# Block inverses of a chunked RWKV-7 recurrence: lower-left parts packed four to a product, and rows taken when a bank is emptied

## The chip, the cores and the metric

The kernel runs on one core of one Trainium2 chip. The metric is the device time of one execution in microseconds. A core has a matrix engine (PE, with its weight loads shown apart as PEld), a vector engine (DVE), a scalar engine (ACT), GpSimd (POOL) and SyncE (SP). PE multiplies a stationary operand of up to 128x128 (the weights) with a moving operand and writes to PSUM, which has eight banks of 128 x 512 fp32 here; the other operands live in SBUF, 128 partitions wide. In this kernel SP does nothing but issue DMAs. Each engine takes its instructions in order.

## What is computed

One step of a hybrid decoder layer on 1024 prompt tokens and 8 sample tokens (one new token each), model width 1024, fp32 throughout. A projection `p = x @ w_in` gives the rows of two branches and their gates. One branch is gated linear attention with 4 heads. The other is RWKV-7 with 16 heads of width 64, a recurrence over tokens:

```
def step(S, inp):
    rt, wt, kt, vt, kkt, at = inp
    sa = einsum('bhvk,bhk->bhv', S, -kkt)
    S = S * wt[:, :, None, :] + sa[..., None] * (kkt * at)[:, :, None, :] + vt[..., None] * kt[:, :, None, :]
    y = einsum('bhvk,bhk->bhv', S, rt)
    return S, y
...
m = sigmoid(gate_a) * (o_gla @ w_up_gla) + sigmoid(gate_b) * (o_rwkv @ w_up_rwkv)
y_out = layernorm(ALPHA * x + m @ w_out)
```

Both branches are normalised and gated before the up-projections, and the new states are outputs too.

## The kernel before

**Two passes.** The tokens are taken in two passes of 512 prompt tokens each (`PASS`); the first also carries the 8 sample tokens (520 columns, as two tiles of 260), the second is one tile of 512. In each pass a long list of *blocks* is worked off (`make_plan`, `blocks`): a block is one 128-column slice of a weight matrix times all tokens of the pass, in 8 slices of depth and three matmuls each (high and low halves of weights and tokens: `whi`, `wlo`, `xh`, `xl`). So a tile of a block is 24 matmuls into one PSUM bank, and the bank is emptied by an *evacuation* (`evacuate`, with the function `ev` that the block's `act` has returned) into a row buffer in SBUF. There are 26 row buffers of 128 x 520, in the pool `row`. Weights are loaded, split on ACT and DVE, and in the first pass their halves are also stored to DRAM, from where the second pass loads them (`load_w`).

**A planner writes the order.** Every piece of work is a generator (a stream) that yields operations or conditions. `Order.run` picks, operation by operation, the one that can start first by its own table of costs and priorities, and emits it; the order on each engine is fixed that way when the kernel is built. `get` and `row` make a stream wait in the planner until a buffer is free: `row(n, KEEP)` waits until one more row is idle than others ask for. Banks are shared out in the same way: two for `proj`, three `big`, one `pch`, two `pY`; up-projections may take any of `proj`, `pY` and `big` (`get_of`).

**Where a block gets its row.** `gla_row` (line 751), `lora` (938), `rwkv_row` (1014) and `gate_row` (1358) are the `act` of a block. Each takes its row before it returns `ev`, and `blocks` (677) runs `act` before the block's first matmul. `up_row` (1392) is the `act` of an up-projection: it waits until a gate has been loaded (`self.gts`, filled by `load_gates`) and takes it off the list, also before the first matmul.

**A pair of heads.** RWKV is worked by pairs of heads, 8 in each pass, 16 in all (`pair`, line 1019): `front`, `back`, `turn`, `chain`, `norm`. Each pass has 8 chunks of 64 tokens (`NCH`). `front` (1034) builds the chunk matrices in `GG` and inverts, for each chunk and head, a unit triangular 64 x 64 matrix. It does so in blocks of 32: the diagonal blocks are written from `GG` to DRAM (`LD`, four DMAs), read back so that each partition holds one block (`L_`, four DMAs named `wide<-LD` in the profile), and solved by 31 steps on DVE (`X`, with `Xt` between). The result goes to DRAM (`XD`, four DMAs) and from there to the diagonal of `XT` (four DMAs, `XT<-XD`). A pair has 8 chunks x 2 heads = 16 such matrices, so 32 solved blocks.

**The lower-left parts.** `back` (1141) computes the off-diagonal block of each inverse from the two diagonal inverses and the off-diagonal block of `GG`, in two rounds of products. The first multiplies, chunk by chunk, the whole of `GG[:, x, 0]` (128 x 128, both heads) with the transposed blocks `X1`; of each result only the rows of interest are copied to `As`. The second multiplies `As` with the other diagonal blocks in `XT`. Each round is 8 products with 128 x 128 weights and 64 moving columns, since a chunk's two heads take two columns of 32 and only one quadrant of 32 partitions of each is used. In the profile the first round has the name `big<-X,gg` and the second `big<-XT,As`. At the end `GG`'s first half is overwritten from `AZ` for `chain`, which runs over the 8 chunks in order.

`X1` and `As` are fixed buffers (line 545), zeroed once at the start, one of each.

Of the kernel before, what the change touches and what calls it, by code (L numbers as in the profile page):

```python
# [20 lines left out]
P = 128  # L21
# [28 lines left out]
    "sto": ([P, P], 1), "bnd": ([P, 1], 3), "st": ([P, 32], 3), "part": ([P, HALF], 2), "l2p": ([P, 2 * P], 2),  # L50
    "pair": ([P, 2, HT // 32], 3),
}
PARTS = ("part", "l2p")
# [29 lines left out]
SETS = {AF.Sigmoid: SIGMOID, AF.Tanh: SIGMOID, AF.Exp: EXP, AF.Ln: EXP}  # L83

HS = (slice(0, 64), slice(64, 128))
LEVELS = [1, 2, 4, 8, 16, 32, 64]
MASKED = 4
GLA_EPS = 1e-5
# [314 lines left out]
class Kern(Order):  # L403
# [71 lines left out]
    def setup(self):  # L475
# [63 lines left out]
        for t in self.Sp:  # L539
            nc.gpsimd.memset(t, 0.0)  # L540

        for tag, n, bufs in (("az", 4 * HT, 2), ("XT", 2 * HT, 2), ("X1", HT, 1), ("As", 2 * HT, 1)):
            ts = [cp.tile([P, n], F32, name=f"{tag}{i}") for i in range(bufs)]
            for t in ts:
                nc.gpsimd.memset(t, 0.0)
            self.fixed(tag, ts)
# [78 lines left out]
    def load_w(self):  # L625

        H = NK // 2
        todo = [(b.src, b.c0, j, b.c.i) for b in self.plan if b.src is not None for j in range(2)]
        raws, his, los, kept = [], [], [], {}

        def keep(src, c0, j, hi, lo):
            for v, x in zip("hl", (hi, lo)):
                t = self.dr.tile([P, 512], F32, name=f"w{v}{c0}_{j}")
                kept.setdefault((c0, j), []).append(t)
                yield self.S.dma_start(t, x.bitcast(F32))

        def high():
            n = 0
            while True:
                yield lambda: len(raws) > n  # L640
                hi = yield from self.get("whi")
                yield self.A.copy(hi, raws[n][0])
                his.append(hi)
                n += 1
                if n == count:
                    return

        def low():
            for n in range(count):
                yield lambda: len(his) > n  # L650
                lo = yield from self.get("wlo")
                raw, src, c0, j, i = raws[n]
                yield self.E.tensor_sub(lo, raw, his[n].bitcast(F32))
                self.free(raw)
                los.append(lo)
                if src is self.a["w_in"] and i == 0:
                    yield from keep(src, c0, j, his[n], lo)
                self.ws.append((his[n], lo))
            self.w_done = True
        count = sum(src is not self.a["w_in"] or i == 0 for src, _, _, i in todo)  # L660
        self.spawn(high(), "w")
        self.spawn(low(), "w")
        for n, (src, c0, j, i) in enumerate(todo):
            if src is self.a["w_in"] and i:
                yield lambda: len(los) == len(raws)
                hi, lo = (yield from self.get("whi")), (yield from self.get("wlo"))
                for x, t in zip((hi, lo), kept[c0, j]):
                    yield self.S.dma_start(x.bitcast(F32), t)
                self.ws.append((hi, lo))
                continue  # L670
            raw = yield from self.get("wraw")
            op = self.S.dma_start(raw.rearrange("p (k c) -> p k c", c=P),
                                  src[j * H * P:(j + 1) * H * P, c0:c0 + P].rearrange("(k p) c -> p k c", p=P))
            yield from self.load(f"w{n}", op)
            raws.append((raw, src, c0, j, i))

    def blocks(self):
        xs = None
        for b in self.plan:
# [5 lines left out]
            if b.src is None:  # L685
                yield from b.act(xs)
                xs = None
                continue
            evac = yield from b.act()
            w = []  # L690
            tiles = b.c.tiles
            for tt, (t0, n) in enumerate(tiles):
# [28 lines left out]
    def low_rank(self, c, raws, used):  # L721
# [26 lines left out]
            c.alr_ready += 1  # L748
        self.free(x_)

    def gla_row(self, c, rows, scale):
        x = yield from self.row(c.n, KEEP)
        rows.append(x)

        def ev(tt, t0, w, q):
            yield self.A.activation(x[:, t0:t0 + w], q, AF.Copy, scale=scale)
        return ev

# [177 lines left out]


    def lora(self, c):
        c.lraw = yield from self.row(c.n)
        return self.shift(c, 32, c.lraw, c.lraw[:, HT:])  # L940

    def lora_done(self, c):
        def parts():
# [40 lines left out]
    def shift(self, c, j, dst, smp):  # L984
# [4 lines left out]
        edge = {}  # L989

        def ev(tt, t0, n, q):
            np_ = n - c.ns if tt == last else n
            yield lambda: "pv" in self.has
# [12 lines left out]
            if prev is not None:  # L1006
                yield V.scalar_tensor_tensor(dst[:, t0:t0 + 1], prev, mu, dst[:, t0:t0 + 1], ALU.mult, ALU.add)
                if not i:
                    self.free(prev)
            if i == 0 and tt == last:  # L1010
                yield V.scalar_tensor_tensor(smp, self.shT[:, j], mu, dst[:, HT:c.n], ALU.mult, ALU.add)
        return ev

    def rwkv_row(self, c, rows, n, p):
        x = yield from self.row(c.n, KEEP)
        rows.append(x)
        return self.shift(c, 8 * n + p, x, self.smp[:, n, p])

    def pair(self, c, p, st, gate):
        d = SimpleNamespace()  # L1020
# [13 lines left out]
    def front(self, c, p, st, d):  # L1034
# [73 lines left out]
        for q in range(2):  # L1108
            b = slice(32 * q, 32 * q + 32)
            for h in range(2):  # L1110
                yield self.S.dma_start(LD[2 * q + h].rearrange("c s t -> s c t"), GG[HS[h]][b, :, 0, h, b])
        L = L_.rearrange("p (s t) -> p s t", t=32)
        X_ = yield from self.get("X")
        X = X_.rearrange("p (i t) -> p i t", t=32)
# [18 lines left out]
        for q in range(2):  # L1133
            b = slice(32 * q, 32 * q + 32)
            for h in range(2):
                n = 2 * q + h
                yield self.S.dma_start(XT[HS[h]][b, :, h, b], XD[n * NCH:(n + 1) * NCH].rearrange("c s t -> s c t"))
        d.AZ, d.BK, d.G, d.XT, d.v, d.bonus, d.pc, d.L = AZ, BK, GG, XT, st[2], st[1], pc, L_
        d.y = Pc_[:, :HT]
# [24 lines left out]

    def turn(self, d):

# [189 lines left out]


    def gate_row(self, c, n, x):
        gt = yield from self.row(c.n, KEEP)

        def ev(tt, t0, w, q):
            yield self.A.copy(gt[:, t0:t0 + w], q)
            if tt == len(c.tiles) - 1:
                yield self.S.dma_start(self.sg[c.i][n][x], gt)
# [225 lines left out]
    def run_all(self):  # L1590
# [4 lines left out]
        self.plan, self.xq, self.ws, self.wo, self.gts = [], [], [], [], []  # L1595
# [65 lines left out]
```

## Time and profile before

| what | value |
|---|---|
| time, median of 3 runs | 1655.22 us (1649.95 to 1656.4) |
| span of the profiled execution, first to last instruction | 1647.8 us |
| mean granted PE clock in it | 0.995 |
| HBM read, written | 195.45 MB, 117.82 MB |
| matmul instructions of the first and of the second round in back | 256 and 256 |

The profile page and all answers of the trace are of one profiled execution. The page gives its span and no time around it, so the runs' times stand beside it and are not of the same execution. In rows of groups, the columns are engine, operation, output and inputs, tile, shape and count, then busy time in us and mean ns of one, then the engine's idle time before them and who ended it. Every instruction that the planner emits has the line of its emitter, L215, so groups go by the names of tiles. Matmul durations overlap their followers; the pace is read from starts. A row of waits is: total us, times, longest us.

### The profile page before, as it was taken

The page shows a single profiled execution, that of the slowest core. Times are in us where ns is not written, and L with a number is a line of the kernel's source. Part 1 is how long each engine was busy: PE and PEld are TensorE (multiplying, and loading weights), DVE is VectorE, ACT ScalarE, POOL GpSimd, SP SyncE. Part 2 cuts the span into 40 slices and gives each one's busy share as a digit, 9 for nine tenths or more (in the row PEclk, how much of TensorE's full clock was granted, in tenths as well). Part 3 has the DMA queues.
Part 4 walks back from the last instruction along what each step waited for, and adds up shares of the span by engine and source line. Part 5 has one row for each costly group of instructions (what it writes and reads, how often), then busy time and mean ns, then how long its engine had stood idle before and what let it go on. Part 6 is the DMA issues. An engine that isn't in the chain of part 4 may idle for free.

```text
span 1647.8 us, 30094 instructions
## 1 busy us (share of the span) xinstructions
PE 1604.5 (97%) x10322; PEld 1422.9 (86%) x10322; DVE 1234.7 (75%) x3187; ACT 844.6 (51%) x2015; POOL 103.3 (6%) x192
## 2 busy tenths in 40 slices
PE   8999999999999999999999999999999999999998
PEld 7899999999999988788878787888788889988786
DVE  6787887788878887768678888796767775665565
ACT  5546755656476646553635462536345645554210
POOL 1100100100000000000001011100000000000000
PEclk9999999999999999999999999999999999999999
DMA  8878764696569655645465546544653577798432
GB/s 281 263 220 254 222 204 149 197 301 198 176 193 280 213 181 189 206 162 145 134 178 162 147 141 193 180 129 125 207 147 106 172 227 228 242 292 264 151 109 84
DMA packets 311925, 315.28 MB, mean 191 GB/s; under 512 B 75364, under 2 KB 197357, under 8 KB 311773
## 3 DMA queue, kind: packets, MB, share of 16 engines
q1 hardware_dynamic: 311772, 313.36, 61.2%
q8 instruction: 82, 1.34, 0.3%
q14 instruction: 71, 0.57, 0.1%
HBM read 195.45 MB, written 117.82 MB: 190 GB/s over the span
## 4 chain that ended last, share of the span: by engine, by line
PE 71%; DVE 13%; DMA 7%; ACT 3%; SPq 3%; issue 2%; POOL 0%; POOLq 0%; DVEq 0%; ACTq 0%
PE proj L215 39%; PE big L215 22%; PE pY L215 7%; PE pch L215 4%; DVE row L215 4%; SPq L215 3%; DVE X L215 2%; DVE Xt L215 2%; DMA wide<-LD 2%; ACT row L215 1%; DVE wide L215 1%; DVE wlo L215 1%; DVE pair L215 1%; DMA whi<-wh 1%; DMA l2s<-lora 1%
## 5 line engine op out<-in xcount | busy, mean ns | idle before, releaser
L215 PE MATMUL proj<-xh,whi 128*128 128x260 f32 (+1 forms) x1872 | 618.2, 330 | 0.1
L215 PE MATMUL proj<-xh,wlo 128*128 128x260 f32 (+1 forms) x1872 | 615.8, 329 | 0.5 <-POOL wlo L215 0.5
L215 PE MATMUL proj<-xl,whi 128*128 128x260 f32 (+1 forms) x1872 | 612.9, 327 | 0.8 <-DVE xl L215 0.7
L215 PEld LDWEIGHTS proj<-xh,wlo 128*128 128x128 f32 x1872 | 354.0, 189 | 28.0 <-issue 5.6
L215 PEld LDWEIGHTS proj<-xh,whi 128*128 128x128 f32 x1872 | 354.7, 189 | 24.7 <-issue 2.3
L215 PEld LDWEIGHTS proj<-xl,whi 128*128 128x128 f32 x1872 | 354.4, 189 | 24.8 <-issue 1.7
L215 ACT CAST whi<-wraw 128x512 fp32r<-128x512 f32 x210 | 130.1, 621 | 92.0 <-PE proj L215 42.3
L215 DVE TENSOR_TENSOR wlo<-wraw,whi 128x512 fp32r<-128x512 f32 x206 | 144.8, 706 | 42.1 <-ACT whi L215 37.3
L215 DVE TENSOR_TENSOR row<-row 128x512 f32<-128x512 f32 (+10 forms) x329 | 164.6, 505 | 11.5 <-PE big L215 4.5
L215 ACT ACTIVATE row<-row 128x512 f32<-128x512 f32 (+5 forms) x229 | 138.5, 610 | 33.2 <-DVE row L215 21.1
L215 ACT ACTIVATE row<-proj,omu 128x260 f32<-128x260 f32 (+1 forms) x99 | 54.2, 547 | 156.0 <-PE proj L215 155.6
L215 DVE TENSOR_TENSOR Xt<-X,wide 128x60 f32<-128x60 f32 (+24 forms) x496 | 108.7, 219 | 30.7 <-DMA wide<-LD 20.0
L215 PE MATMUL big<-row 128*128 128x64 f32 (+4 forms) x712 | 115.7, 281 | 6.5 <-DVE row L215 5.9
L215 DVE TENSOR_TENSOR X<-X,Xt 128x60 f32<-128x60 f32 (+24 forms) x496 | 107.4, 217 | 11.5
L215 ACT ACTIVATE s0p<-wide,pc 64x64 f32<-64x64 f32 x256 | 88.1, 344 | 43.4 <-DVE wide L215 39.1
L215 PEld LDWEIGHTS big<-row 128*128 128x128 f32 (+1 forms) x712 | 96.8, 191 | 15.5 <-DVE row L215 10.7
L215 DVE SCALAR_TENSOR_TENSOR wide<-pch,pc,s0p 64x64 f32<-64x64 f32 x224 | 63.1, 282 | 56.7 <-PE pch L215 52.2
L215 ACT COPY wide<-pch 64x64 f32<-64x64 f32 x230 | 47.3, 206 | 105.0 <-PE pch L215 101.6
L215 POOL TENSOR_TENSOR row<-row 128x512 f32<-128x512 f32 (+5 forms) x40 | 47.9, 1198 | 715.2 <-ACT row L215 210.8
L215 DVE SCALAR_TENSOR_TENSOR row<-proj,pv,row 128x259 f32<-128x259 f32 (+1 forms) x99 | 56.4, 570 | 40.5 <-ACT tail L215 23.7
L215 ACT COPY row<-big 128x128 f32<-128x128 f32 (+7 forms) x163 | 45.8, 307 | 52.4 <-PE big L215 51.3
L215 PE MATMUL big<-az,wide 128*128 128x256 f32 x256 | 66.7, 383 | 0.3 <-DVE gg L215 0.2
(256 smaller groups left out, 2714.5 us busy)
## 6 DMA issues: line engine op xcount, KB each, us to landing
wraw<-w_in SPq DMA_DIRECT2D x146, 256.0 KB
wh<-whi SPq DMA_DIRECT2D x146, 256.0 KB
wl<-wlo SPq DMA_DIRECT2D x146, 256.0 KB
whi<-wh SPq DMA_DIRECT2D x146, 256.0 KB
wlo<-wl SPq DMA_DIRECT2D x146, 256.0 KB
wide<-LD SPq DMA_DIRECT2D x64, 128.0 KB
wraw<-w_up_gla SPq DMA_DIRECT2D x32, 256.0 KB
wraw<-w_up_rwkv SPq DMA_DIRECT2D x32, 256.0 KB
```

The costliest lines, as they stand in the source:

```text
L215: ways.append((eng, lambda call=call: call(out, *args, **kw), price(eng, name, out, args, ins)))
```

## The change

**Packing.** Two new buffers: `Lp`, 128 x 512 (one, fixed and zeroed at the start), and `Xs`, 128 x 384 (one). `As` is half as wide, `X1` goes. Four lower-left blocks (two chunks x two heads, one in each quadrant of partitions) make one product now: `Lp` holds the off-diagonal blocks of `GG` along a diagonal, four to each of its four 128 x 128 matrices, brought there by four DMAs from `GG` in `front`, just behind the LD writes. `Xs` holds the diagonal inverses in the same packing, brought by eight DMAs from `XD`, behind the four XT loads. `back` transposes 128 columns of `Xs` once, multiplies `Lp` with the result in 4 products of 32 columns, copies the four quadrants to the diagonal of `As`, multiplies in 4 products of 32 columns, and copies the four quadrants to `XT`. `Lp` is taken in `front` and freed in `back` behind the first round; `Xs` is taken in `front` and freed at the end of `back`. The copies from `AZ` into `GG` stay.

**Rows and gates.** `act` no longer waits. The row is taken in `ev` at the block's first tile (`landing`), that is when the first bank is to be emptied; the evacuation of a second tile waits until the row is there. `up_row` notes its place in the order of up-projections, and its evacuation waits until that many gates are loaded.

**A list append.** In `load_w`, `los.append(lo)` comes behind the stores of the split weights and the entry in `ws`, and no longer ahead of them.

```diff
-        for tag, n, bufs in (("az", 4 * HT, 2), ("XT", 2 * HT, 2), ("X1", HT, 1), ("As", 2 * HT, 1)):
+        for tag, n, bufs in (("az", 4 * HT, 2), ("XT", 2 * HT, 2), ("Lp", HT, 1), ("As", HT, 1)):
...
-                los.append(lo)
                 if src is self.a["w_in"] and i == 0:
                     yield from keep(src, c0, j, his[n], lo)
                 self.ws.append((his[n], lo))
+                los.append(lo)
...
-            evac = yield from b.act()
+            evac = b.act()
...
+    def landing(self, c, rows, tt):
+
+        if tt:
+            yield lambda: rows[0] is not None
+        else:
+            rows[0] = yield from self.row(c.n, KEEP)
+        return rows[0]
+
     def gla_row(self, c, rows, scale):
-        x = yield from self.row(c.n, KEEP)
-        rows.append(x)
+        at = [None]
 
         def ev(tt, t0, w, q):
+            x = yield from self.landing(c, at, tt)
+            if not tt:
+                rows.append(x)
             yield self.A.activation(x[:, t0:t0 + w], q, AF.Copy, scale=scale)
...
+        Lp = (yield from self.get("Lp")).rearrange("p (y t) -> p y t", t=P)
+        for n, b in enumerate(QS):
+            h = n % 2
+            yield self.S.dma_start(Lp[b, :, b], GG[QS[2 * h], n // 2::2, 0, h, 32:64])
...
+        Xs = yield from self.get("Xs")
+        xp = Xs[:, :2 * P].rearrange("p (q y t) -> p q y t", q=2, t=32)
+        for n, b in enumerate(QS):
+            for q in range(2):
+                u = (2 * q + n % 2) * NCH + n // 2
+                yield self.S.dma_start(xp[b, q], XD[u:(2 * q + n % 2 + 1) * NCH:2].rearrange("c s t -> s c t"))
...
-        X1_, As_ = (yield from self.get("X1")), (yield from self.get("As"))
-        X1 = X1_.rearrange("p (c h t) -> p c h t", c=NCH, h=2)
-        As = As_.rearrange("p (c h t) -> p c h t", c=NCH, h=2)
-        q = [slice(32 * n, 32 * n + 32) for n in range(4)]
-        for h in range(2):
-            yield self.V.transpose(X1[q[2 * h], :, h], XT[q[2 * h], :, h, 0:32])
-        pA = yield from self.bank("big", [P, NCH, 2, 32])
-        for x in range(NCH):
-            yield self.P.matmul(pA[:, x], GG[:, x, 0], X1[:, x], start=True, stop=True)
-        for h in range(2):
-            yield self.C.copy(As[q[2 * h + 1], :, h, 0:32], pA[q[2 * h + 1], :, h])
-        self.free(pA, X1_)
-        pZ = yield from self.bank("big", [P, NCH, 2, 32])
-        for x in range(NCH):
-            yield self.P.matmul(pZ[:, x], As[:, x], XT[:, x, :, 32:64], start=True, stop=True)
-
+        As_ = yield from self.get("As")
+        As = As_.rearrange("p (y t) -> p y t", t=P)
+        X1, X2 = (d.Xs[:, n * P:(n + 1) * P].rearrange("p (y t) -> p y t", t=32) for n in (2, 1))
+        yield self.V.transpose(d.Xs[:, 2 * P:3 * P], d.Xs[:, 0:P])
+        pA = yield from self.bank("big", [P, NCH // 2, 32])
+        for y in range(NCH // 2):
+            yield self.P.matmul(pA[:, y], d.Lp[:, y], X1[:, y], start=True, stop=True)
+        for b in QS:
+            yield self.C.copy(As[b, :, b], pA[b])
+        self.free(pA, d.Lp)
+        pZ = yield from self.bank("big", [P, NCH // 2, 32])
+        for y in range(NCH // 2):
+            yield self.P.matmul(pZ[:, y], As[:, y], X2[:, y], start=True, stop=True)
+        for n, b in enumerate(QS):
+            h = n % 2
+            yield self.C.copy(XT[QS[2 * h], n // 2::2, h, 32:64], pZ[b])
         for h, hs in enumerate(HS):
-            yield self.C.copy(XT[q[2 * h], :, h, 32:64], pZ[q[2 * h], :, h])
             yield self.C.copy(GG[hs, :, 0, h], d.AZ[hs, :, 0, h])
-        self.free(pZ, As_)
+        self.free(pZ, As_, d.Xs)
...
     def up_row(self, c, n, x):
-        yield lambda: self.gts
-        gt, m = self.gts.pop(0)
+        place = len(self.asked)
+        self.asked.append(x)
 
         def ev(tt, t0, w, q):
             s = slice(t0, t0 + w)
+            yield lambda: len(self.gts) > place
+            gt, m = self.gts[place]
```

`lora`, `rwkv_row` and `gate_row` are changed as `gla_row` is: `landing` gives the row to `ev`, and for the first two it is handed on by a function argument of `shift`.

More of the change, by code (lines that the diff above doesn't have):

```diff
@@ L49 @@
     "Xt": ([P, P], 1), "S": ([P, GDV], 2), "s0p": ([P, C], 2), "rh": ([P, P], 2),
-    "sto": ([P, P], 1), "bnd": ([P, 1], 3), "st": ([P, 32], 3), "part": ([P, HALF], 2), "l2p": ([P, 2 * P], 2),
+    "sto": ([P, P], 1), "Xs": ([P, 3 * P], 1), "bnd": ([P, 1], 3), "st": ([P, 32], 3), "part": ([P, HALF], 2), "l2p": ([P, 2 * P], 2),
     "pair": ([P, 2, HT // 32], 3),
@@ L85 @@
 HS = (slice(0, 64), slice(64, 128))
+QS = tuple(slice(32 * n, 32 * n + 32) for n in range(4))
 LEVELS = [1, 2, 4, 8, 16, 32, 64]
@@ L938, in lora, with to @@
     def lora(self, c):
-        c.lraw = yield from self.row(c.n)
-        return self.shift(c, 32, c.lraw, c.lraw[:, HT:])
+        def to(x):
+            c.lraw = x
+        return self.shift(c, 32, to, None)
     def lora_done(self, c):
@@ L982, in tails, with shift @@
             self.free(st_)
-    def shift(self, c, j, dst, smp):
+    def shift(self, c, j, to, smp):
         i, A, V = c.i, self.A, self.V
@@ L988, in shift @@
         last = len(c.tiles) - 1
-        edge = {}
+        edge, at = {}, [None]
         def ev(tt, t0, n, q):
             np_ = n - c.ns if tt == last else n
+            dst = yield from self.landing(c, at, tt)
+            if not tt:
+                to(dst)
             yield lambda: "pv" in self.has
@@ L1010, in ev @@
             if i == 0 and tt == last:
-                yield V.scalar_tensor_tensor(smp, self.shT[:, j], mu, dst[:, HT:c.n], ALU.mult, ALU.add)
+                yield V.scalar_tensor_tensor(dst[:, HT:c.n] if smp is None else smp, self.shT[:, j], mu, dst[:, HT:c.n],
+                                             ALU.mult, ALU.add)
         return ev
     def rwkv_row(self, c, rows, n, p):
-        x = yield from self.row(c.n, KEEP)
-        rows.append(x)
-        return self.shift(c, 8 * n + p, x, self.smp[:, n, p])
+        return self.shift(c, 8 * n + p, rows.append, self.smp[:, n, p])
     def pair(self, c, p, st, gate):
@@ L1137, in front @@
                 yield self.S.dma_start(XT[HS[h]][b, :, h, b], XD[n * NCH:(n + 1) * NCH].rearrange("c s t -> s c t"))
+        Xs = yield from self.get("Xs")
[4 more added lines that the diff above has]
+                yield self.S.dma_start(xp[b, q], XD[u:(2 * q + n % 2 + 1) * NCH:2].rearrange("c s t -> s c t"))
         d.AZ, d.BK, d.G, d.XT, d.v, d.bonus, d.pc, d.L = AZ, BK, GG, XT, st[2], st[1], pc, L_
+        d.Lp, d.Xs = Lp, Xs
         d.y = Pc_[:, :HT]
@@ L1358, in gate_row @@
     def gate_row(self, c, n, x):
-        gt = yield from self.row(c.n, KEEP)
+        at = [None]
         def ev(tt, t0, w, q):
+            gt = yield from self.landing(c, at, tt)
             yield self.A.copy(gt[:, t0:t0 + w], q)
@@ L1594, in run_all @@
         self.sampled = self.w_done = False
-        self.plan, self.xq, self.ws, self.wo, self.gts = [], [], [], [], []
+        self.plan, self.xq, self.ws, self.wo, self.gts, self.asked = [], [], [], [], [], []
         self.setup()
```

## The prediction

> **What bounds the kernel now.** I read the page's busy shares first, then busy time by stage, then what the matrix engine (PE) waited for. The page begins:
>
> ```profile
> span 1647.8 us, 30094 instructions
> PE 1604.5 (97%) x10322; PEld 1422.9 (86%) x10322; DVE 1234.7 (75%) x3187; ACT 844.6 (51%) x2015; POOL 103.3 (6%) x192
> PE 71%; DVE 13%; DMA 7%; ACT 3%; SPq 3%; issue 2%; POOL 0%; POOLq 0%; DVEq 0%; ACTq 0%
> ```
>
> The busy line is enough to see that PE leaves only 1647.8 - 1604.5 = 43.3 us of the span; the last line is the chain that ended last, and 71% of it is PE. A busy PE can still hide slack, so the stages come next (window, then busy time and count of PE, weight loads, DVE, ACT, POOL, then clock, DMA share, GB/s):
>
> ```profile
> 0.00:100.00 100.00, 94.34 (x704) 84.45 (x705) 74.09 (x167) 49.12 (x111) 14.90 (x32) 1.00 0.83 264
> 100.00:700.00 600.00, 587.03 (x4550) 557.81 (x4549) 484.87 (x1343) 365.25 (x932) 34.82 (x72) 1.00 0.69 212
> 760.00:1300.00 540.00, 529.11 (x2873) 442.64 (x2872) 416.97 (x1171) 260.51 (x631) 44.73 (x69) 1.00 0.50 153
> 1300.00:1460.00 160.00, 154.24 (x1083) 142.08 (x1082) 113.40 (x260) 89.59 (x180) 1.95 (x6) 0.98 0.78 241
> 1460.00:1648.00 188.00, 180.07 (x800) 145.69 (x799) 105.99 (x166) 45.92 (x86) 2.77 (x3) 0.99 0.52 167
> ```
>
> In both projection stages (100 to 700 and 760 to 1300) PE is busy 98% of the time at full clock. Those are the stages in which the pairs run, so a matmul that disappears there leaves a gap that the next projection matmul can fill. PE's waits, longest first in total, tell what little is left:
>
> ```profile
> PE big L215 <- DVE row L215: 6.3, 9, 1.5
> PE pch L215 <- DVE wide L215: 5.4, 7, 1.5
> PE pch L215 <- DVE rh L215: 5.2, 12, 0.7
> PE big L215 <- DMA row<-xT: 5.2, 2, 4.4
> PE big L215 <- DVE l2p L215: 3.3, 3, 1.8
> ...
> PE proj L215 <- POOL wlo L215: 0.5, 1, 0.5
> ...
> PE big L215 <- DVE gg L215: 0.2, 1, 0.2
> ```
>
> The first matmuls' wait for x (5.2 us) is start-up. The rest are waits for the pairs' and heads' own operands; a weight (wlo) was late once, by 0.5 us.
>
> **Part 1: fewer products.** Now two rounds of 8 products per pair invert the lower-left blocks; after, two rounds of 4. Their rows on PE, by form, and one round in the timeline with the matmuls around it:
>
> ```profile
> L215 PE MATMUL big<-X,gg 128*128 128x64 f32 x256 | 31.2, 271 | 0.8 <-DVE X L215 0.5 <-ACT row L215 0.3
> L215 PE MATMUL big<-XT,As 128*128 128x64 f32 x256 | 30.8, 272 | 1.0 <-ACT As L215 1.0
> ...
> 208.12 1.89 PE L215 MATMUL big<-X,gg 128*128 128x64 f32 x16
> 209.82 0.37 PE L215 MATMUL proj<-xh,wlo 128*128 128x260 f32 x1
> ...
> 510.82 0.51 PE L215 MATMUL big<-row 128*128 128x8 f32 x4
> 511.19 0.36 PE L215 MATMUL proj<-xh,whi 128*128 128x260 f32 x1
> ```
>
> 256 instructions in 16 pairs is 16 per round of 8 products: one fp32 product is two instructions. The durations of 271 ns overlap, so the price is the pace: the next matmul starts 209.82 - 208.12 = 1.70 us after the round's first, 0.106 us an instruction. A pair spends 2 x 1.70 = 3.40 us. After, it issues 2 x 8 = 16 instructions with 32 moving columns, a form that the trace lacks. Bounds: the 64-column pace above and the 8-column one, (511.19 - 510.82) / 4 = 0.0925. A pair then costs 1.48 to 1.70 us, and 16 pairs save **27.2 to 30.7 us**. I take 27.2: 64 to 8 columns moves the pace so little that columns hardly count.
>
> The Trainium skill ("TensorE: Matmul & The Clock Gate", LDWEIGHTS) prices a weight load by its columns alone, columns / 1.2 ns. By it, as an estimate, 128 columns cost 107 ns whatever the moving width, and the sum would be 27.3 us; the 64-column row agrees, the 8-column row is 13% below it.
>
> **Part 2: evacuations and transposes.** Their rows on ACT and DVE, with the nearest smaller and larger forms:
>
> ```profile
> L215 ACT COPY As<-big 32x256 f32<-32x256 f32 x32 | 11.7, 365 | 19.1 <-PE big L215 18.6
> L215 ACT COPY XT<-big 32x256 f32<-32x256 f32 x30 | 10.9, 362 | 17.3 <-PE big L215 17.0
> L215 ACT COPY row<-big 32x128 f32<-32x128 f32 x16 | 4.1, 256 | 7.9 <-PE big L215 7.8
> L215 DVE STREAM_TRANSPOSE X<-XT 32x256 f32<-32x256 f32 x32 | 13.8, 431 | 2.5 <-DMA XT<-XD 2.0
> L215 DVE STREAM_TRANSPOSE row<-row 128x512 f32<-128x512 f32 x16 | 11.3, 705 | 0.0
> ```
>
> Four copies of 32x128 replace two of 32x256, twice: 8 x 0.256 - 2 x (0.365 + 0.362) = +0.59 us a pair on ACT or DVE. One transpose of 128 columns replaces two of 256: from 256 to 512 columns it grows by 274 ns, so 128 columns are near 431 - 137 = 294 ns, and 2 x 0.431 - 0.294 = 0.57 us goes. These cancel. ACT, at 51%, covers 16 x 0.59 = 9.4 us; without that cover it would be the whole 9.4. The copies of AZ into GG stay.
>
> **Part 3: twelve more DMAs a pair on SP.** Four load Lp just behind the four LD writes, eight load Xs behind the four XT loads. The same kinds today, in SP's timeline (with the pair's first round on PE ahead of it), then SP's longest waits, then the queue's line on the page:
>
> ```profile
> 132.07 1.89 PE L215 MATMUL big<-X,gg 128*128 128x64 f32 x16
> ...
> 118.21 3.23 SPq L215 DMA_DIRECT2D XD<-X  x4
> ...
> 124.90 2.43 SPq L215 DMA_DIRECT2D XT<-XD  x4
> ...
> 148.59 1.80 SPq L215 DMA_DIRECT2D LD<-gg  x4
> 150.50 0.40 SPq L215 DMA_DIRECT2D row<-state_gla  x1
> 150.99 0.41 SPq L215 DMA_DIRECT2D row<-vd  x1
> 153.63 1.72 SPq L215 DMA_DIRECT2D wide<-LD  x4
> ...
> SPq L215 <- PE proj L215: 270.9, 134, 7.3
> SPq L215 <- ACT whi L215: 99.6, 49, 9.6
> ...
> q1 hardware_dynamic: 311772, 313.36, 61.2%
> ```
>
> An issue takes 1.80 / 4 = 0.45 to 2.43 / 4 = 0.61 us: 5.4 to 7.3 us a pair, 86 to 117 us of SP in all. What stands behind them on SP is the weight traffic. The cover is that SP is early: 270.9 us of it go in 134 waits until a projection has read a weight buffer, and of the 153.63 - 150.39 = 3.24 us between its LD writes and the loads of LD two other issues take 0.81, and in the 2.4 us left most of the Lp issues fit. The eight Xs loads put 3.6 to 4.9 us between the solve and the products; part 1 gives back 1.7 of it inside back. The next pair's LD writes came at 148.59, 15 us behind the first round of this pair (132 to 134), so Lp, one buffer now held from front to back, is free in time; its wait on SP is long over when reached. Bounds for part 3: 0 and 117 us. I take **4 us**, because PE waited 0.5 us for a weight in the whole run, and because SP's waits for PE say that weights are early rather than late.
>
> The DMA engines get 12 x 128 runs of 128 bytes a pair, 24,576 in all. Today's mean packet takes 0.612 x 1647.8 x 16 / 311772 = 51.8 ns; at that price they add 24,576 x 51.8 ns / 16 = 80 us of each engine, 4.8% of the span, on 61.2%.
>
> **Part 4: rows and gates at the emptying of the bank.** Before, a block of projections did not start until a row was free (an up-projection until its gate was loaded). After, its matmuls go ahead and the evacuation takes the row. No instruction is added or dropped; at run time ACT's first copy waits for the row's last reader, with the pairs' ACT copies queued behind it, and the bank (two of proj) is held meanwhile. The gain can be no more than PE's waits without the start-up: 34.6 - 5.2 = 29.4 us, where 34.6 is the sum of all eighteen of them, from 6.3 down to 0.2. The loss: if late evacuations doubled the three waits for DVE's row, wide and rh, 6.3 + 5.4 + 5.2 = 16.9 us. I take a gain of **3 us**: PE is already 98% busy, so rows seldom held it up. Moving one list append behind the weight stores reorders two SP issues at most, nothing.
>
> **Sum.** -27.2 + 0 + 4 - 3 = -26.2 us, a span of 1621.6. The profile gives no time around its span; the median of the runs, 1655.22, is 7.4 us above it, the lowest, 1649.95, 2.1. With the same 7.4 the forecast is **1629 us** (-1.6%). A measurement can tell about 0.5% from no change: faster means below 1647, slower above 1663.
>
> **The rivals.**
>
> *Rows were the limit* (0.13). If the scattered waits come from blocks held back by a row, two fifths of the 29.4 go, 12 us in place of 3: 1620 us, and with the 8-column pace 1616. For it: in each such wait PE had no projection to do. Against: that may as well be order, since each wait is short (at most 1.8 us).
>
> *Half the saving stays idle* (0.16). In pass 1 (760 to 1300) DVE is busy 77% and PE waits for the chain's DVE steps. If the 8 pairs of that pass give idle for busy, 8 x 1.70 = 13.6 us are lost: 1643, and with part 3 at 10 us in place of 4, 1649: around the bound between faster and same. Against it: 98% busy in that stage means that projections do fill gaps.
>
> *The weights come late in pass 0* (0.09), the slower end. There SP also stores the split weights, and the DMA share is 0.69 with 0.83 at the start. If SP's bursts delay weight loads by their full length, PE starves 6.4 us (the middle of 5.4 and 7.3) in each of 8 pairs: 1629 - 4 + 51 = 1676. It decides from 3.3 us of starving a pair in pass 0 on: that eats 26 us. Against it: one late weight of 0.5 us, and 270.9 us of SP waiting for PE. The Trainium skill speaks for this rival ("DMA: Bandwidth & Descriptors", Specifications): transfers below 512 bytes are read, modified and written. Were the new 128-byte packets twice as dear by it, that share would be, as an estimate, 9.7% of the engines and not 4.8; no row shows such packets by themselves.
>
> *The change doesn't do what it says* would mean that part 4 moves nothing, since blocks wait for weights or banks: 1632 us, inside the forecast's range.
>
> **How the numbers follow.** The forecast has 0.62 (own range 1621 to 1640). Faster: 0.62 + 0.13 + half of 0.16 = 0.83; same 0.08; slower 0.09. The range runs from 1613 (rows, the 8-column pace and 3 us less for part 3) to 1647 (the forecast with part 4 at its loss, 16.9, in place of a gain); it leaves out the dear end of part 3 and part of the second rival, under 2 in 10.
>
> **What would show it.** Right: the X,gg and XT,As groups at half their count, replaced by Lp and Xs groups of 128x32 whose rounds last about 0.85 us from first start to the next matmul; PE busy near 1577 us and still 97%; no new wait of PE for a weight. Part 3 wrong: PE waits for whi or wlo, or SP's waits for proj melt by far more than 86 us. Part 4 wrong: ACT waits in front of copies from proj. The prediction fails if the 32-column pace is above 0.106 us, or if PE's idle time grows by what its busy time loses.

## The result and the profile after

The changed kernel takes 1629.28 us, median of 4 runs (1623.61 to 1630.32), against 1655.37 (4 runs) for the kernel before. The ratio is 0.9857, 95% interval 0.9836 to 0.9878. The forecast was 1629. On a second chip the ratio was 0.9839 (0.982 to 0.9858). The total hides that two of the steps behind it were put wrongly; the experiments below show which.

The page of the changed kernel begins:

```profile
span 1627.4 us, 29876 instructions
PE 1579.8 (97%) x10066; PEld 1394.6 (86%) x10066; DVE 1226.9 (75%) x3201; ACT 844.6 (52%) x2054; POOL 92.3 (6%) x185
q1 hardware_dynamic: 339420, 316.52, 62.9%
```

PE has 256 instructions fewer, its busy time fell by 1604.5 - 1579.8 = 24.7 us, and its idle time (span less busy) rose from 43.3 to 47.6, by 4.3. 24.7 - 4.3 is the 20.4 us between the two spans. The new rounds, in the groups by form and then one round in PE's timeline with the matmul behind it:

```profile
L216 PE MATMUL big<-Xs,Lp 128*128 128x32 f32 x128 | 16.0, 267 | 1.1 <-DVE Xs L216 0.9
L216 PE MATMUL big<-Xs,As 128*128 128x32 f32 x128 | 15.7, 266 | 0.2 <-ACT As L216 0.2
...
133.43 0.97 PE L216 MATMUL big<-Xs,Lp 128*128 128x32 f32 x8
134.24 0.37 PE L216 MATMUL proj<-xh,wlo 128*128 128x260 f32 x1
```

A round takes PE 134.24 - 133.43 = 0.81 us, 0.101 us an instruction. Against 1.70 us before, that is 2 x 0.89 x 16 = 28.5 us of PE. Busy time fell by less, and the clock dipped more often in this execution. In steps of 10 us, summing 10 us x (1 - granted clock) over the steps below full clock, without the last step of the span, gives 6.8 us before and 10.2 after; -28.5 + 3.4 = -25.1, beside the 24.7 measured. The sum is an upper value for what the clock cost, as part of a slow step can be idle. On the second chip the changed kernel's profile has 6.8 us of such loss again, as before, and there busy time is 1575.0, 29.5 less than before, and the span 1620.0.

What PE waited for after, longest first (total, times, longest):

```profile
PE big L216 <- DMA row<-xT: 7.1, 3, 4.0
PE pch L216 <- DVE wide L216: 6.2, 7, 2.0
PE pch L216 <- DVE rh L216: 4.5, 5, 1.5
PE big L216 <- DVE part L216: 3.2, 7, 0.9
PE proj L216 <- DMA whi<-wh: 3.1, 2, 2.5
PE big L216 <- DVE row L216: 1.8, 3, 0.9
...
PE proj L216 <- DMA wlo<-wl: 1.0, 1, 1.0
...
PE big L216 <- DVE Xs L216: 0.9, 1, 0.9
```

Two of the new waits matter for what follows: those for stored weights (whi, wlo) on their way back, 4.1 us together, and one for Xs, 0.9 us. The rise of 4.3 us in idle time is the net of these and of older waits that grew (DVE's part, 0.3 to 3.2) or shrank (DVE's row, 6.3 to 1.8).

### The profile page after: what moved, and what is told of

It reads as the page before. It is cut to its first block, busy times and chain, and to the rows that moved or that the text cites. A ratio compares the mean times of both kernels' runs of the same rounds, so it can differ in the third digit from the quotient of the medians.

```text
span 1627.4 us, 29876 instructions
## 1 busy us (share of the span) xinstructions
PE 1579.8 (97%) x10066; PEld 1394.6 (86%) x10066; DVE 1226.9 (75%) x3201; ACT 844.6 (52%) x2054; POOL 92.3 (6%) x185
## 4 chain that ended last, share of the span: by engine, by line
PE 71%; DVE 12%; DMA 6%; SPq 4%; ACT 3%; issue 2%; POOL 0%; POOLq 0%; DVEq 0%; ACTq 0%
PE proj L216 41%; PE big L216 20%; PE pY L216 6%; SPq L216 4%; PE pch L216 4%; DVE row L216 4%; DVE X L216 2%; DVE wide L216 2%; DVE Xt L216 1%; DMA wide<-LD 1%; ACT row L216 1%; DMA wlo<-wl 1%; DVE wlo L216 1%; DMA row<-xT 1%; DMA row<-o_gla 1%
## 5 line engine op out<-in xcount | busy, mean ns | idle before, releaser
L216 DVE TENSOR_TENSOR row<-row 128x512 f32<-128x512 f32 (+9 forms) x334 | 164.1, 498 | 11.7 <-ACT row L216 4.2
L216 DVE TENSOR_TENSOR wlo<-wraw,whi 128x512 fp32r<-128x512 f32 x205 | 141.3, 692 | 39.4 <-ACT whi L216 35.8
L216 ACT ACTIVATE row<-row 128x512 f32<-128x512 f32 (+4 forms) x229 | 138.1, 610 | 38.1 <-DVE row L216 28.7
L216 DVE TENSOR_TENSOR Xt<-X,wide 128x60 f32<-128x60 f32 (+24 forms) x496 | 105.1, 212 | 43.2 <-DMA wide<-LD 32.4
L216 ACT ACTIVATE row<-proj,omu 128x260 f32<-128x260 f32 (+1 forms) x99 | 54.3, 548 | 137.9 <-PE proj L216 137.2
L216 DVE TENSOR_TENSOR X<-X,Xt 128x60 f32<-128x60 f32 (+24 forms) x496 | 105.0, 212 | 12.5
L216 PEld LDWEIGHTS big<-row 128*128 128x128 f32 (+1 forms) x712 | 98.1, 192 | 12.5 <-DVE row L216 4.6
L216 POOL TENSOR_TENSOR row<-row 128x512 f32<-128x512 f32 (+5 forms) x35 | 38.2, 1092 | 580.7 <-ACT row L216 188.7
```

Source lines behind the costliest of these rows:

```text
L216: ways.append((eng, lambda call=call: call(out, *args, **kw), price(eng, name, out, args, ins)))
```

## The experiments

Theory A was that of the prediction: PE is the limit, products pay their issue pace, loads are nearly free, late rows give little. As it fell in part, theories D and E came up; they are stated with the runs. Each run stands beside runs of the kernel before on the same chip. Ratios are to the kernel before; span, PE busy, idle (their difference) and the wait of PE for Xs are those of the run's profile. Clock loss is the sum described above. All executions of a kernel run the same order, which is fixed when it is built; the profile is of one of them. Each run is described below.

| run | ratio (95%) | span | PE busy | PE idle | waits for Xs | clock loss |
|---|---|---|---|---|---|---|
| before | 1 | 1647.8 | 1604.5 | 43.3 | none | 6.8 |
| changed | 0.9857 (0.9836 to 0.9878) | 1627.4 | 1579.8 | 47.6 | 0.9 | 10.2 |
| after_again, second chip | 0.9839 (0.982 to 0.9858) | 1620.0 | 1575.0 | 45.0 | 1.8 | 6.8 |
| pack_only | 1.0014 (0.9997 to 1.003) | 1646.8 | 1585.2 | 61.6 | 14.6 | 20.4 |
| rows_only | 1.0007 (0.9988 to 1.0025) | 1645.7 | 1599.9 | 45.8 | none | 5.1 |
| pack_rows | 0.9911 (0.9894 to 0.9929) | 1631.8 | 1578.9 | 52.9 | 9.0 | 15.5 |
| pack_gates | 0.9956 (0.994 to 0.9973) | 1641.2 | 1585.2 | 56.0 | 8.1 | 16.7 |
| pack_late | 1.0123 (1.0104 to 1.0142) | 1667.8 | 1594.6 | 73.2 | 15.8 | 29.0 |
| pack_first | 0.9919 (0.9895 to 0.9943) | 1635.4 | 1577.9 | 57.5 | 1.4 | 13.6 |
| first | 0.9894 (0.9876 to 0.9911) | 1631.6 | 1577.3 | 54.3 | 2.0 | 9.9 |
| other_order | 0.9987 (0.9972 to 1.0002) | 1641.8 | 1576.6 | 65.2 | 7.0 | 14.7 |
| before_other_order | 0.9944 (0.9923 to 0.9965) | 1643.7 | 1600.3 | 43.4 | none | 14.3 |
| prod_twice | 1.0109 (1.0081 to 1.0137) | 1655.5 | 1607.5 | 48.0 | 1.1 | 12.0 |
| loads_twice | 1.1816 (1.1793 to 1.184) | 1943.9 | 1666.6 | 277.3 | 57.6 | 174.0 |

### The parts by themselves: pack_only and rows_only

The edits have many lines, and the cut shows one of each. Edit of pack_only: the changed kernel with `gla_row`, `lora`, `shift`, `rwkv_row`, `gate_row`, `up_row`, `load_w` and `blocks` as before. Edit of rows_only: the kernel before with those functions, and `landing`, as after.

```diff
# pack_only
-            evac = b.act()
+            evac = yield from b.act()
# rows_only
-            evac = yield from b.act()
+            evac = b.act()
```

> The packing with its twelve loads, and none of the late rows, late gates or the moved append. Theory A (PE is the limit; products pay their issue pace, loads are nearly free, late rows give little): 23 to 28 us faster than before, 1627 to 1632 us. Theory B (the rows were the limit and half of the packing's gain stays idle): 10 to 15 us faster, 1640 to 1645.

> Late rows, late gates and the moved append on the kernel before, without the packing. Theory A: 0 to 5 us faster than before, 1650 to 1655 us. Theory B: 10 to 15 us faster, 1640 to 1645, and PE's waits for DVE shrink by about as much.

Neither moved the time: 1.0014 and 1.0007, both intervals around 1. That refutes A for pack_only (it asked for 1627 to 1632; the median was 1650.85 beside 1649.64) and B for both. The two parts add up to nothing, and the whole gives 1.4 to 1.6%. Where did the packing's saving go? In pack_only PE's busy time did fall, by 19.3 us, but its idle time rose by 18.3. That is a sign of failing that the prediction had named, though for the changed kernel. PE's waits in that run begin:

```profile
PE big L216 <- DVE Xs L216: 14.6, 4, 7.7
PE big L216 <- DMA row<-xT: 5.2, 3, 4.1
```

Three of the four waits for Xs make up nearly all of the 14.6 us: two in pass 0 and the longest, 7.7 us, at the last pair. Those of pass 0, with the transpose ahead of the first:

```profile
371.54 0.29 DVE L216 STREAM_TRANSPOSE Xs<-Xs 128x128 f32<-128x128 f32 x1
...
371.89 1.92 PE L216 MATMUL big<-Xs,Lp 128*128 128x32 f32 x8 [3.33 <-DVE Xs L216]
545.63 1.92 PE L216 MATMUL big<-Xs,Lp 128*128 128x32 f32 x8 [3.30 <-DVE Xs L216]
```

The transpose at 371.54 has no idle time ahead of it: DVE had other work up to then. The last packet of the Xs loads (each load moves 128 packets of 128 bytes) had ended at 370.95. So in pass 0 the late loads and DVE's own order end close together, and the trace does not put that stall down to the loads alone. At the last pair it does. There SP's timeline, DVE's and PE's, each with the idle time ahead of an instruction and its cause in brackets, and then busy time in steps of 10 us:

```profile
1354.29 1.99 SPq L216 DMA_DIRECT2D XT<-XD  x4
1356.33 3.46 SPq L216 DMA_DIRECT2D Xs<-XD  x6
1359.90 0.36 SPq L216 DMA_DIRECT2D mg<-row  x1
1360.30 1.88 SPq L216 DMA_DIRECT2D row<-o_rwkv  x4
1362.22 0.91 SPq L216 DMA_DIRECT2D Xs<-XD  x2
...
1366.32 0.31 DVE L216 STREAM_TRANSPOSE Xs<-Xs 128x128 f32<-128x128 f32 x1 [6.10 <-DMA Xs<-XD]
...
1366.68 1.92 PE L216 MATMUL big<-Xs,Lp 128*128 128x32 f32 x8 [7.73 <-DVE Xs L216]
...
1350.00:1360.00 10.00, 8.96 (x75) 8.75 (x73) 6.51 (x12) 3.55 (x6) 0.00 (x0) 1.00 0.64 167
1360.00:1370.00 10.00, 2.17 (x10) 2.03 (x10) 1.25 (x4) 1.03 (x4) 0.00 (x0) 0.55 0.93 289
1370.00:1380.00 10.00, 10.00 (x69) 10.00 (x70) 1.41 (x3) 6.56 (x18) 0.00 (x0) 0.77 0.51 195
```

The last two Xs loads stand behind four loads of o_rwkv and are issued at 1362.22, 8 us behind the first XT load. The transpose waits for them on DVE until 1366.32, and the products stand on PE for 7.73 us with everything behind them; the clock is at 0.55 in the step that holds most of this and at 0.77 in the next. The changed kernel has nearly the same order on SP (first XT load at 1343.42, last Xs loads at 1351.01), and from the first XT load to the transpose it takes the same 12.03 us. But in its order PE has other matmuls ahead of the products until 1354.90, 11.5 us behind the first XT load; in pack_only they end at 1358.96, 4.7 us behind it. So PE stands for 0.92 us only:

```profile
1351.01 1.27 SPq L216 DMA_DIRECT2D Xs<-XD  x3
...
1355.45 0.31 DVE L216 STREAM_TRANSPOSE Xs<-Xs 128x128 f32<-128x128 f32 x1 [2.66 <-DMA wraw<-w_up_gla]
...
1355.82 1.08 PE L216 MATMUL big<-Xs,Lp 128*128 128x32 f32 x8 [0.92 <-DVE Xs L216]
```

The view puts the transpose's wait there down to a load of w_up_gla; the last packet of Xs had ended at 1354.58.

So two theories. **D**: late rows give PE projections to do while a pair waits for its packed blocks, and so belong to the gain. **E**: the order that the planner happened to write put products ahead of the arrival of their blocks; any other order may avoid it.

### The price of products and of loads: prod_twice and loads_twice

```diff
# prod_twice, and the same for the second round
-            yield self.P.matmul(pA[:, y], d.Lp[:, y], X1[:, y], start=True, stop=True)
+            for _ in range(2):
+                yield self.P.matmul(pA[:, y], d.Lp[:, y], X1[:, y], start=True, stop=True)
# loads_twice, and the same for Lp
-                yield self.S.dma_start(xp[b, q], XD[...])
+                for _ in range(2):
+                    yield self.S.dma_start(xp[b, q], XD[...])
```

> The changed kernel with each of its eight products a pair issued twice (16 more instructions a pair, 256 in all, into the same place). Theory A: PE is full, so each adds its pace of 0.101 us: 26 us over the changed kernel, 1655 us. Theory B (half of it falls into idle time): 13 us over, 1642.

> The changed kernel with each of the twelve packing loads issued twice (192 more DMAs on SP). Theory A: SP is early, so 0 to 6 us over the changed kernel, 1629 to 1635 us. Rival C (weights come late behind SP's bursts): 20 us or more over, 1650 and up, with PE waiting for whi and wlo.

In prod_twice PE's busy time is 1607.5, 27.7 above the changed kernel's first profile and 32.5 above its second, about the 26 us that the doubled instructions cost at 0.101. The profiles' spans differ by 28.1 and 35.5. But the profiled execution is the fastest of six, 1657.32 us. The median is 1668, 1.1% above the kernel before, so by the ratios the doubled products cost 42 to 45 us and not A's 26. The order does not explain the rest: it is the same in all six, and in the profile PE is idle for 48.0 us, as in the changed kernel. Four of the five longer executions had a lower granted clock (0.985 to 0.988, against 0.991); no profile shows more. So PE's busy time bears A out, and the time only in part.

loads_twice failed as a price for a load. A doubled load writes the same place as the first, and SP stood on the loads' landing. SP's longest waits:

```profile
SPq L216 <- PE proj L216: 228.9, 100, 6.8
SPq L216 <- DMA Xs<-XD: 167.9, 120, 3.6
SPq L216 <- DMA Lp<-gg: 84.6, 64, 2.9
```

What it shows instead is that SP must not stand: with 167.9 + 84.6 = 252.5 us of waiting for these loads on SP the kernel was 18% slower, PE waited 61.5 us for whi and 57.6 for Xs, and the mean clock was 0.910. Rival C's signs came, but by SP standing and not by the length of its bursts. In the changed kernel SP's wait for PE has shrunk from 270.9 to 220.6 us. The price of the twelve loads by themselves was not measured.

### Rows or gates: pack_rows and pack_gates

pack_rows is the changed kernel with `up_row` as before (`blocks` then takes both kinds of `act`); pack_gates is pack_only with the late `up_row`. The list append is as after in pack_rows, as before in pack_gates.

```diff
# pack_rows: the gate is taken ahead of the matmuls again
-        place = len(self.asked)
-        self.asked.append(x)
+        yield lambda: self.gts
+        gt, m = self.gts.pop(0)
```

> The changed kernel itself once more, beside the kernel before on this chip, so that parts and whole are compared on one chip. All theories: 0.983 to 0.988 of the kernel before. The packing alone was 1.001 of it and the late rows alone 1.001, so the whole is more than its parts; the next three runs are to say where that comes from.

> The packing with late rows, but with gates taken before the matmuls as in the kernel before. Theory D (late rows keep PE supplied while a pair waits for its packed blocks): 0.983 to 0.990 of the kernel before, as the whole. Theory E (the packing alone lost its gain by an accident of order, in single waits for the late packed blocks, and any other order may avoid them): anywhere from 0.983 to 1.002, following the sum of PE's waits for Xs, which was 14.6 us in the packing alone and 0.9 in the changed kernel.

> The packing with late gates, but with rows taken before the matmuls as in the kernel before. Theory D: near the packing alone, 0.997 to 1.002 of the kernel before. Theory E: anywhere from 0.983 to 1.002, by the sum of PE's waits for Xs.

0.9911 and 0.9956: between the packing alone and the whole, each with one or more stalls on Xs. pack_rows has the stall at the last pair, 9.0 us; pack_gates has two of 3.3 us at 371 and 545 us. D asked for the whole's ratio in pack_rows and for no gain in pack_gates, and missed both, if narrowly.

```profile
1350.25 1.91 PE L216 MATMUL big<-Xs,Lp 128*128 128x32 f32 x8 [8.98 <-DVE Xs L216]
```

```profile
371.12 1.91 PE L216 MATMUL big<-Xs,Lp 128*128 128x32 f32 x8 [3.32 <-DVE Xs L216]
544.73 1.76 PE L216 MATMUL big<-Xs,Lp 128*128 128x32 f32 x8 [3.31 <-DVE Xs L216]
```

With pack_only (on another chip) and the changed kernel these two make a comparison of two by two. The two stalls of 3.3 us in pass 0 are in both kernels that take rows early (pack_only, pack_gates) and in neither that takes them late. The stall of 7.7 or 9.0 us at the last pair is in both that take gates early (pack_only, pack_rows); with late gates it is 0.9 us (pack_gates, the changed kernel). The times follow: beside the packing, late rows with the append are worth 1.0 to 1.2% of the kernel before (1.0014 to 0.9911, 0.9956 to 0.9839) and late gates 0.6 to 0.7% (1.0014 to 0.9956, 0.9911 to 0.9839). So with this constant of the planner D is right in kind, for gates as well as rows. Each of the four has its own order, though, and that rows and gates as such did it is not shown; another constant is tried below.

### The planner told that Xs is later: pack_late

```diff
         d.Lp, d.Xs = Lp, Xs
+        t, by = self.ready[Xs.tensor.name]
+        self.ready[Xs.tensor.name] = t + 2.5, by
```

> The packing alone, with the planner told that Xs lands 2.5 us later than it reckons, so that the transpose and the products stand later in the order; nothing else is changed. Theory D: no late rows, so no gain, 0.997 to 1.002 of the kernel before. Theory E: the waits for Xs go (from 14.6 us to under 3), and with them the loss: 0.983 to 0.990.

A miss for both theories: 1.0123. The waits for Xs did not go (15.8 us), and idle time rose to 73.2 us. At the last pair SP's loads stand in the same order as in pack_only, the transpose comes 12.5 us behind the first XT load, and PE stands for 9.1 us; a new stall of 4.5 us came at 209.75. Shifting a due time in the planner is no clean way to test a wait: it changes everything else with it.

### The loads earlier: pack_first and first

The blocks are stored in another order in LD and XD, so that one load can fill a quadrant of Xs where two were needed, and the four loads stand ahead of the XT loads. pack_first does this to pack_only, first to the changed kernel.

```diff
-                yield self.S.dma_start(LD[2 * q + h]...
+                yield self.S.dma_start(LD[2 * h + q]...
...
+        xs = Xs[:, :2 * P].rearrange("p (y t) -> p y t", t=32)
+        for n, b in enumerate(QS):
+            u = 2 * (n % 2) * NCH + n // 2
+            yield self.S.dma_start(xs[b], XD[u:2 * (n % 2 + 1) * NCH:2].rearrange("c s t -> s c t"))
         for q in range(2):
             b = slice(32 * q, 32 * q + 32)
             for h in range(2):
-                n = 2 * q + h
+                n = 2 * h + q
```

> The packing alone (rows and gates as in the kernel before), with Xs filled by four loads in place of eight, issued ahead of the four XT loads. Theory E (in the packing alone PE stood for Xs, whose eight loads come last on SP): PE's waits for Xs go from 14.6 us to under 4, the time to 0.983 to 0.990 of the kernel before. Theory D (late rows are needed for the gain, whatever the loads do): 0.997 to 1.002.

> The changed kernel with Xs filled by four loads ahead of the XT loads. Theory E: 0.980 to 0.985 of the kernel before, since PE stands for Xs only 0.9 to 1.8 us in the changed kernel and little is left to win; 64 issues fewer on SP. Theory D: the same, 0.982 to 0.986.

In pack_first the waits for Xs went from 14.6 to 1.4 us, as E asked, and without late rows the time went to 0.9919. D's 0.997 to 1.002 is refuted: late rows are not needed for a gain when the loads come earlier. But E's 0.983 to 0.990 was missed, as other waits came in: 4.4 us for the first xh of the up-projections, 2.9 us for a part. In the changed kernel the same edit made it worse, 0.9894 beside 0.9839 to 0.9857, missing both expectations: the waits for Xs had been small there, and waits for the chain (pch) and for DVE's row and l2p grew. PE's waits in first:

```profile
PE pch L216 <- DVE wide L216: 9.5, 10, 2.0
PE big L216 <- DVE row L216: 7.0, 8, 1.5
PE big L216 <- DMA row<-xT: 5.3, 2, 4.0
PE big L216 <- DVE l2p L216: 4.2, 5, 1.6
```

No run beat the changed kernel.

### The same work in another order: other_order and before_other_order

One constant of the planner's costs is altered; what is computed, loaded and stored stays.

```diff
-HOLD = 0.11
+HOLD = 0.12
```

> The changed kernel with one constant of the planner's costs at 0.12 in place of 0.11: the same work, another order on every engine. Theory E (the changed kernel's order happens to miss the waits for Xs): anywhere from 0.984 to 1.0 of the kernel before, by PE's waits for Xs. Theory D (late rows cover the waits in any order): 0.982 to 0.987, waits for Xs under 3 us.

> The kernel before with the same planner constant at 0.12 in place of 0.11: the same work, another order on every engine. The changed kernel lost 1.4% by this. Theory F (the order alone moves either kernel by ten or twenty us, through single waits): 1.005 to 1.015 of the kernel before, PE's idle time 10 us or more above its 43. Theory G (only the packed kernel is so touchy, since its products hang on loads that come last on SP): 0.997 to 1.003, idle time as before.

The changed kernel fell to 0.9987: almost the whole gain lost, with late rows in place, by an order with one stall of 6.3 us on Xs and one of 5.9 us on xh:

```profile
375.21 1.92 PE L216 MATMUL big<-Xs,Lp 128*128 128x32 f32 x8 [6.27 <-DVE Xs L216]
...
1330.14 0.58 PE L216 MATMUL pY<-xh,whi 128*128 128x260 f32 x1 [5.94 <-ACT xh L216]
```

That refutes D's 0.982 to 0.987 and fits E. E's range was wide, though, and its measure is not enough: with 7.0 us of waits for Xs this run is slower than pack_rows with 9.0. At 375.21 the transpose had again followed DVE's other work without a pause (374.85), with the last packet of Xs ended at 373.96. The kernel before moved the other way, to 0.9944, and its idle time stayed at 43.4 us. So F failed in sign, and G held for idle time and missed for the time. Under this constant the packed kernel is the slower of the two, 0.9987 beside 0.9944. Why the kernel before gained is not shown: in its profile PE's busy time is 4.2 us lower at a clock loss 7.5 us higher. The changed kernel's gain of 1.4 to 1.6% belongs to its order with the one constant; no third was tried.

## Why the prediction was right, and where it was not

**What bounds the kernel: right.** In the eight kernels with single rounds and single loads PE's busy time lies 9.9 (pack_late, with 29.0 us of clock loss) to 29.5 us below the kernel before's; where the clock loss was equal (after_again) it is 29.5 below. The saving of PE's work is there in every order.

**Part 1: right.** 32 columns run at 0.101 us an instruction, inside 0.0925 to 0.106; 28.5 us where 27.2 was taken. The prediction's estimate of 107 ns was 6% too high.

**Part 2: right.** The copies take 0.257 us (0.256 taken) and the transpose 0.305 (0.294 taken):

```profile
L216 ACT COPY As<-big 32x128 f32<-32x128 f32 x60 | 15.4, 257 | 14.2 <-PE big L216 13.6
L216 DVE STREAM_TRANSPOSE Xs<-Xs 128x128 f32<-128x128 f32 x16 | 4.9, 305 | 6.2 <-DMA Xs<-XD 3.5 <-DMA wraw<-w_up_gla 2.7
```

PE's waits for the copies' results (As and XT) are 1.6 us after and 1.0 before, near the 0 that was taken.

**Part 3: near in size for this order, wrong as a step.** Idle time rose by 4.3 us where 4 was taken, but that is the net of all waits. The sign that the prediction gave for this part being wrong, PE waiting for whi or wlo, did come: 4.1 us, in after_again 2.9. The larger omission is another. The prediction named the 3.6 to 4.9 us that the Xs loads put between the solve and the products, and gave them no price. The delay came as said: from the issue of the first XT load to the transpose it is 4.2 us before and 7.8 after, as medians of 16 pairs, and at the last pair 4.5 and 12.0. What it costs hangs on whether PE has other work ahead of the products in its order. In the changed kernel PE waited 0.9 and 1.8 us for Xs, in prod_twice 1.1; in the five other orders with the same eight loads it was 7.0 to 15.8 us, with slow clock behind it. The range of 0 to 117 us would have held that; the value was read from one trace's slack.

The DMA engines bore less than was estimated. The prediction gave the new packets 51.8 ns each, 80 us of each engine; in the traces a packet of 128 bytes takes 12.8 ns before (49,152 of them) and 12.6 after (24,576 more), so they take 19 us of each engine.

**Part 4: the step that failed.** It gave 3 us to late rows by themselves, and they gave nothing (1.0007, 0.9988 to 1.0025). Beside the packing late rows and gates came with 1.6 to 1.75%, from pack_only's 1.0014 to the changed kernel's 0.9857 and 0.9839. The sum treated the four parts as independent. They aren't: the stalls that late rows and gates take away are there only with the packing, and the order is written anew for each edit. How much of the effect belongs to late rows and gates as such, and how much to the order they happen to lead to, stays open, since other_order has both and lost as much to other stalls. The moved append was not tried alone.

**The base, and luck.** The 7.4 us between the profiled span and the median were not time outside the span. For the changed kernel each run's time is 1.8 us above its own span (1629.18 and 1627.4). So the profile of before was of a short run; if the same 1.8 us holds, of the one of 1649.95. The sum of -26.2 agrees with the medians (-26.1) and the shortest runs (1649.95 to 1623.61, -26.3), not with the two spans (-20.4), between which the clock loss differs by 3.4 us. The total came within 0.3 us partly by luck. The rounds saved 1.3 us more than was taken, and idle time rose by 4.3 us (1.7 on the second chip) where parts 3 and 4 together made it 1. Above all, the order that the planner happened to write is one that nearly misses the stalls; with the constant at 0.12 the same forecast would have been some 1.4% too low. The upper end of the range, 1647, does not follow from its own terms: 1629 + 3 + 16.9 is 1649.

**The rivals.** The rows were not the limit. A large part of the saving staying idle is what the variants show: idle time is 9.6 us above the kernel before's in pack_rows, 12.7 in pack_gates, 18.3 in pack_only and 21.9 in other_order, beside 28.5 saved. The mechanism was not the chain in pass 1 but mainly single waits for Xs in either pass. Waits for late weights were 4.1 us.

## What to carry to other kernels

Here work taken off a full engine paid at its issue pace only where that engine had something else to do until the new operands came, 3.6 us later than the old ones at the median pair. So ask of each product which load or copy stands last before it, on which queue that stands behind others, and what the engine has ahead of it meanwhile. Where a planner writes the whole order anew, try parts and whole in more than one order before an effect of 1% is given to a part: here one constant of 0.01 us moved the same work by 1.3 to 1.5%. A forecast can hit the total while two of its terms are wrong.

## What was not expected of the hardware

The clock can drop at short gaps, though not at each. In the changed kernel a gap of 2.04 us at 1054.78 stands in a step of 10 us at a clock of 0.83, in the kernel before one of 1.48 us at 925.08 in a step at 0.85; but a gap of 1.82 us at 613.95 in the kernel before left the clock at 1.00 from 612 to 618 us. What decides it is not shown. The slow stretch is short and deep: 0.52 from 1056.0 to 1059.3 us behind the first, 0.50 from 927.0 to 930.4 behind the second. Behind the longer stall of 3.33 us in pack_only it is 0.51 from 371.0 to 381.2, and around the 7.73 us it is 0.50 from 1360.9 to 1374.4. Steps of the changed kernel and of the kernel before:

```profile
1050.00:1060.00 10.00, 7.96 (x35) 6.47 (x35) 6.10 (x22) 3.74 (x10) 0.00 (x0) 0.83 0.70 219
```

```profile
920.00:930.00 10.00, 8.52 (x40) 7.01 (x38) 9.12 (x33) 0.89 (x3) 1.28 (x1) 0.85 0.48 143
```

So a stall can be paid twice. pack_only has 18.3 us more idle time than the kernel before, and 13.6 us more clock loss. Part of that loss lies in the idle time itself; PE's busy time fell by 19.3 us where the rounds save 28.5, so 9.2 us of it can be seen there. The Trainium skill ("TensorE: Matmul & The Clock Gate", What's actually happening) ties the drop to an idle window of about 3.4 us; the gaps in the two steps shown are shorter, and the rows decide.

A small load took long to land: the last two Xs loads of pack_only, of 16 KB each, were issued from 1362.22 on, their first packet moved at 1364.76 and their last ended at 1365.67, and they held the transpose until 1366.32, at a DMA share of 0.93 in that step.
